# A decoder trunk: the second norm's steps directly behind the first's, one norm computed early, a normalization beside down products, and weights fetched by half units

## The chip, the cores and the metric

The kernel runs on one core of one Trainium2 chip. The metric is the time of one execution on the device in microseconds (us). TensorE (PE) multiplies matrices; VectorE (DVE), ScalarE (ACT) and GpSimd (POOL) work on elements; SyncE (SP) issues the DMAs. Each engine runs its own instructions in program order and waits where another engine's result is missing. Matrix products end up in PSUM, which has 8 banks here; everything else lies in SBUF. [...]

## The reference

One layer of a hybrid decoder, over 1072 positions (16 learned meta tokens, 1024 of the prompt, 32 of the samples), 1024 channels and a hidden width of 2816:

```python
def rmsnorm(x, g):
    y = xf * lax.rsqrt(jnp.mean(xf * xf, axis=-1, keepdims=True) + EPS)
    return (y * g.astype(jnp.float32)).astype(x.dtype)
...
def swiglu(x, wg, wu, wd):
    return (jax.nn.silu(x @ wg) * (x @ wu)) @ wd
...
    x = x + 0.5 * swiglu(rmsnorm(x, g1), w1g, w1u, w1d)
    h = rmsnorm(x, gm)
    z = h @ w_in + b_in
...
    x = x + jnp.concatenate([c, q], axis=-1) @ w_out + b_out
    x = x + 0.5 * swiglu(rmsnorm(x, g2), w2g, w2u, w2d)
```

Here c is a causal convolution over positions and q a pooling over several widths, both of z. A last norm follows.

## The kernel before

Channels lie on the partitions, positions along the rows. The positions are cut into three pieces of 358: X1, X2 and X3. Every value that is multiplied is split into a high part (a cast on ACT, `hi`) and the remainder (a subtraction, `lo`); a product is then three matmuls (high by high, low by high, high by low), which `mul` issues and `split` prepares. So every operand costs one ACT and one DVE (or POOL) instruction, and all weights go through ACT and POOL. In the rows, a name that ends in h or l is such a part (b11h, b11l).

TensorE's order is the order in which the program is written. `plan` is a list of steps: each takes its weights (`take`, `unit`) and issues products. Work of the other engines that doesn't belong to a step (norms, splits of operands, the mixing) is written as generators, which stand in a queue (`launch`); after each step some of their parts are issued, in order, and a part that ends in `yield LAG` lets that much of TensorE's time pass before the next. The order on DVE, ACT and POOL is then set by a scheduler, under the order of dependent work.

The stages:

1. Start (to about 80 us). The first two hidden tiles of FFN1 for X1 and X2 are computed before the norm is known: products run on x times the gain (`parts`, `product`), and the factor 1/rms is applied behind. Class `Start` writes this by hand. `rsqrt` is the norm: three column sums on TensorE (rows `ones,ns`), twelve tiny DVE instructions, a diagonal matrix `diag` on DVE, three matmuls with it that spread the factor over all partitions into a PSUM bank, and a copy `nr` of it. The products are named (0,0) to (0,3) for X1 and (1,0) to (1,3) for X2 (two of `g`, two of `u`). After them, `first_blocks`, `differences` and `last_blocks` make the seven operands b11 to b22 of the next stage.
2. FFN1 for X1 and X2 by "fast" blocks: seven products in place of eight, as in Strassen's scheme, on sums of weights (`block_steps`, tile `sx`) and sums of operands. Pairs of hidden tiles go through `fast_pass`; at pairs 1, 3, 5 and 7 groups of two pairs begin, whose down products (`fast_down`) are fast too, and whose ends load DVE heavily.
3. FFN1 for X3 (`plain_pass`, to about 850 us) and, with it, the first mixing. Its input is X3's norm (`rms`, 8 squares on ACT and 7 adds on DVE) and 8 scaled tiles in `normed` (tile `smt`).
4. FFN2 for X1's part (340 positions), with the second mixing between its steps, and from about 1260 us `fast_operands`: the norms of X2 and X3 and 60 DVE instructions that make the seven operands of
5. FFN2 for X2 and X3 by fast blocks, and the last norm.

Raw weights come by DMA in units of 512 KB (`raw_tile`, four buffers); `take` hands out a unit and keeps two more requested. A fast block uses two units: the first is split at once and kept; `sums` adds and subtracts the halves of both in four DVE instructions.

Of the kernel before, what the change touches and what calls it, by code (L numbers as in the profile page):

```python
# [13 lines left out]
P = 128  # L14
# [40 lines left out]
LAG4 = 7.0  # L55
POOL = {'b1': (1, 3), 't4': (0, 1, 2, 3), 't3': (0, 1, 2, 3), 't2': (1, 3), 'sq': ()}
W_BUFS = 6
T_BUFS = 6
R_BUFS = 4
# [22 lines left out]
def trunk(ctx: ExitStack, tc: tile.TileContext, xt, wf1, win, wout, wf2, wpool, vec, eye, sconv, spool,  # L82
# [64 lines left out]
    def raw_tile():  # L147
        return const.tile([P, KD, P], F32, name="wraw", tag="wraw", bufs=R_BUFS)

    def fetch(n):  # L150
        while len(fetched) < n and state["raw"] < len(raw_list):
            raw = raw_tile()
            for at, src in raw_list[state["raw"]]:
                to = at + src.shape[-1] // P
                nc.sync.dma_start(raw[:, at:to].rearrange("p k m -> p (k m)"), src)
# [15 lines left out]
    def unit(raw):  # L171
        return half_unit(raw[:, :KH]), half_unit(raw[:, KH:])
# [11 lines left out]
    def rsqrt(src, scale, add, out=None, copied=True):  # L184
# [22 lines left out]
        yield LAG2  # L207
# [63 lines left out]
    def fast_operands(pieces, gain, out):  # L271


        st = {}
# [7 lines left out]
        yield from rms(p0, st)  # L282
        yield from rms(p1, st)
        for k in range(KH):
            b11, b21, b12, b22, t3 = (temp()[:, :n] for _ in range(5))
            scaled(b11, p0, k, gain, st[p0])
            scaled(b21, p0, KH + k, gain, st[p0])
            yield
            put("b11", k, b11)
            put("b21", k, b21)  # L290
            yield
            scaled(b12, p1, k, gain, st[p1])
            scaled(b22, p1, KH + k, gain, st[p1])
            yield
            nc.vector.tensor_tensor(t3, b22, b12, ALU.subtract)
            nc.vector.tensor_tensor(b12, b12, b11, ALU.subtract)
            yield
            put("t1", k, b12)
            put("t3", k, t3)
            put("b22", k, b22)  # L300
            yield
            nc.vector.tensor_tensor(b22, b22, b12, ALU.subtract)
            put("t2", k, b22)
            yield
            nc.vector.tensor_tensor(b21, b21, b22, ALU.subtract)
            put("t4", k, b21)
            yield

    class Start:
# [4 lines left out]
        def __init__(self, pieces, gain, out, hid):  # L314
            self.pieces, self.gain, self.st = pieces, gain, {}
            self.n = pieces[0][1] - pieces[0][0]
            self.ops = out["ops"] = operand_tiles(self.n)
            self.accs, self.hid, self.sums, self.steps = {}, hid, {}, {}

# [25 lines left out]
        def norms(self, c):  # L345

            if c not in self.steps:
                self.steps[c] = rsqrt(self.sums[c], 1.0 / D, EPS)
                next(self.steps[c])
            else:  # L350
                self.st[c] = whole(self.steps[c])

        def after(self, c, j):

            if (c, j) == (0, 0):
                self.square_sums(0)
            elif (c, j) == (0, 1):
                self.norms(0)
                self.parts(1)
            elif (c, j) == (0, 2):  # L360
                self.square_sums(1)
            elif (c, j) == (0, 3):
                self.norms(0)
                self.outputs(0)
                self.first_blocks()
            elif (c, j) == (1, 0):
                self.norms(1)
            elif (c, j) == (1, 2):
                self.norms(1)
                self.differences()  # L370
            elif (c, j) == (1, 3):
                self.outputs(1)
                self.last_blocks()
                rest_of_start()

        def outputs(self, c):
            r = self.st[c]
            for i in range(2):
                t = pools["fast"].tile([P, self.n], F32, name="cc", tag="cc", bufs=4)
# [4 lines left out]
                if i not in self.hid:  # L384
                    fa1_places(0)
                split(self.hid[i][0][c], self.hid[i][1][c], t)
# [58 lines left out]
    def down_steps(wsrc, p, pieces, hid):  # L445
        out = []
        for j in range(2):
# [10 lines left out]
            out.append(("step", [source], lambda: unit(take()), use, False))  # L458
        return out

    def plain(src, use):
        return ("step", [[(0, src)]], lambda: unit(take()), use, False)
# [26 lines left out]
    def block_steps(src0, src1, product):  # L489
# [3 lines left out]
        def make0():  # L493
            st["r0"] = take()
            return unit(st["r0"])
# [5 lines left out]
        def sums():  # L501
            if "m5" not in st:
                r0, r1 = st["r0"], take()
                s1 = pools["fast"].tile([P, KH, P], F32, name="sx", tag="sx", bufs=2)
                nc.vector.tensor_tensor(s1, r1[:, :KH], r1[:, KH:], ALU.add)  # L505
                nc.vector.tensor_tensor(r1[:, :KH], r0[:, :KH], r1[:, :KH], ALU.subtract)  # L506
                nc.vector.tensor_tensor(r0[:, :KH], s1, r0[:, :KH], ALU.subtract)  # L507
                nc.vector.tensor_tensor(r0[:, KH:], r0[:, KH:], r0[:, :KH], ALU.subtract)
                st.update(m5=s1, m6=r0[:, :KH], m7=r1[:, :KH], m3=r0[:, KH:], m4=r1[:, KH:])
# [489 lines left out]
    r1b = {}  # L999
# [12 lines left out]
    def open_mix():  # L1012
# [10 lines left out]
        raw = raw_tile()[:, :C_TILES]  # L1023
# [36 lines left out]
    def fast_pass(pairs, downs, before, pieces, first):  # L1060
# [4 lines left out]
        for p, (g, u) in enumerate(pairs):  # L1065
# [24 lines left out]
            if p == 2:  # L1090
                do(launch, "twist", twist(pieces))
            elif p - 1 == last:
# [24 lines left out]
    def to_second_piece():  # L1117
# [3 lines left out]
        finish("h1b")  # L1121

    do(to_second_piece)
    put_down(fa1_d[PAIRS - 2])

# [6 lines left out]
    plain_pass(fb1, fb1_d, fa1_d[PAIRS - 1], {  # L1132
# [8 lines left out]
    def to_last():  # L1141
# [3 lines left out]
        launch("s2", fast_operands(FFN2_B, "g2", box["s2"]))  # L1145
# [5 lines left out]
            lambda: do(launch, "cb", mixer(MIX_B, lambda: both("small", n_b1, "sm"), box["cb"], lambda: cbs["b"]))],  # L1151
# [40 lines left out]
    def last_downs(c, j):  # L1192
# [19 lines left out]
        return ("step", raws, lambda: (unit(take()), unit(take())), use, False)  # L1212
# [17 lines left out]
    for p in steps:  # L1230
        raw_list.extend(p[1])
    raw_list[0] = [(at, raw_list[0][0][1][:, at * P : (at + KH) * P]) for at in (0, KH)]
# [4 lines left out]
    fetch(1)  # L1237
    for k in range(1, KD):
        start.load(0, k)
    fetch(2)  # L1240
    for k in range(KD):
        start.load(1, k)
        if k == 3:
            fetch(3)
# [111 lines left out]
```

## Time and profile before

| | |
|---|---|
| time, median of 3 runs | 1847.15 us (1845.55 to 1848.17) |
| the profiled execution | 1845.23 us, of which the span is 1843.5 us |
| busy: PE, DVE, ACT, POOL | 1747.4 us (95%), 1400.9 (76%), 761.2 (41%), 1154.1 (63%) |
| granted clock of TensorE, mean | 0.973 |

The span is the time from the first to the last recorded instruction. [...] A matmul of 358 columns is recorded with its whole passage (some 330 ns), while the next enters about 165 ns behind it.

### The profile page before, as it was taken

Reading aid. Unit: us, or ns where it says so; the run is one execution under the profiler, and the core shown is the slowest. Engines: PE = TensorE matmul, PEld = TensorE weight load, DVE = VectorE, ACT = ScalarE, POOL = GpSimd, SP = SyncE. Lnnn points to the kernel's source line nnn. Section 1 sums busy time; section 2 is a strip of 40 time slices with the busy share of each in tenths; the row PEclk is TensorE's granted clock in tenths of the full one; section 3 lists DMA queues with packets and bytes.
Section 4 is the critical chain, followed back from the end, with each engine's and each line's share of the span. In section 5 each row is a group of like instructions: output and inputs, shape, how many; then the busy total and the mean of one; then the engine's idle time right before and its main releaser. Section 6 shows DMA issues by size and latency. Waiting matters only on the chain.

```text
span 1843.5 us, 29182 instructions
## 1 busy us (share of the span) xinstructions
PE 1747.4 (95%) x10486; PEld 1726.9 (94%) x10486; DVE 1400.9 (76%) x2621; ACT 761.2 (41%) x1482; POOL 1154.1 (63%) x894
## 2 busy tenths in 40 slices
PE   8699999999899999999999999999799999999997
PEld 7699999999799999999999999999699899989997
DVE  8979797989746696898235888537878888797965
ACT  6434444444424324434235433535453434434344
POOL 6576766667635336667246658665577676766683
PEclk9799999999999999999999999999899999999998
DMA  6022222222243223343224493443233222222222
GB/s 204 24 74 78 78 69 69 79 73 95 97 91 119 76 70 101 129 135 118 69 93 136 120 139 127 137 137 120 87 92 94 74 70 69 82 77 72 69 92 87
DMA packets 74560, 176.17 MB, mean 96 GB/s; under 512 B 23728, under 2 KB 30128, under 8 KB 74416
## 3 DMA queue, kind: packets, MB, share of 16 engines
q1 hardware_dynamic: 74416, 174.31, 31.3%
q8 instruction: 83, 1.36, 0.3%
q14 instruction: 61, 0.50, 0.1%
HBM read 169.13 MB, written 5.15 MB: 95 GB/s over the span
## 4 chain that ended last, share of the span: by engine, by line
PE 72%; DVE 18%; issue 5%; DMA 3%; POOL 2%; ACT 1%; SPq 0%; DVEq 0%; POOLq 0%; ACTq 0%
PE acc L123 72%; DMA wraw<-in_wf 3%; POOL wl L141 2%; DVE acc L245 2%; DVE acc L535 1%; DVE wraw L506 1%; DVE tmp L535 1%; DVE acc L779 1%; DVE tmp L245 1%; DVE tmp L657 1%; DVE wraw L507 1%; DVE sx L505 0%; DVE x L456 0%; DVE dt4l L141 0%; DVE xk L245 0%
## 5 line engine op out<-in xcount | busy, mean ns | idle before, releaser
L141 POOL TENSOR_TENSOR wl<-wraw,wh 128x512 fp32r<-128x512 f32 x740 | 996.3, 1358 | 598.2 <-ACT wh L140 567.6
L140 ACT CAST wh<-wraw 128x512 fp32r<-128x512 f32 x740 | 453.9, 620 | 687.9 <-PE acc L123 465.6
L123 PE MATMUL acc<-smt,wh 128*128 128x358 f32 x1024 | 252.8, 328 | 4.5 <-DVE mixl L141 2.2
L123 PEld LDWEIGHTS acc<-smt,wh 128*128 128x128 f32 x1024 | 181.8, 190 | 5.8 <-DVE mixl L141 2.5
L779 DVE SCALAR_TENSOR_TENSOR acc<-ub,vecs,acc 128x340 f32<-128x340 f32 (+2 forms) x348 | 183.7, 573 | 2.7
L123 PE MATMUL acc<-mixlt,wh 128*128 128x340 f32 x704 | 167.0, 321 | 4.9 <-DVE smt L141 2.4
L123 PE MATMUL acc<-smt,wl 128*128 128x358 f32 x512 | 167.8, 328 | 0.0
L456 DVE SCALAR_TENSOR_TENSOR x<-acc,x 128x358 f32<-128x358 f32 (+1 forms) x240 | 119.5, 518 | 38.8 <-PE acc L123 38.1
L583 DVE SCALAR_TENSOR_TENSOR x<-acc,x 128x358 f32<-128x358 f32 x320 | 144.9, 518 | 0.2 <-PE acc L123 0.2
L123 PEld LDWEIGHTS acc<-mixlt,wh 128*128 128x128 f32 x704 | 121.9, 190 | 6.0 <-DVE smt L141 2.7
L535 DVE TENSOR_TENSOR acc<-tmp,acc 128x358 f32<-128x358 f32 x168 | 85.3, 527 | 51.3 <-PE acc L123 45.8
L141 POOL TENSOR_TENSOR wl<-sx,wh 128x512 fp32r<-128x512 f32 x58 | 86.0, 1484 | 49.1 <-ACT wh L140 46.8
L123 PE MATMUL acc<-mixlt,wl 128*128 128x340 f32 x352 | 112.8, 320 | 0.8 <-POOL wl L141 0.8
L123 PEld LDWEIGHTS acc<-smt,wl 128*128 128x128 f32 x512 | 96.9, 189 | 0.0
L505 DVE TENSOR_TENSOR sx<-wraw 128x512 f32<-128x512 f32 x58 | 62.4, 1076 | 38.5 <-DMA wraw<-in_wf 38.3
L507 DVE TENSOR_TENSOR wraw<-sx,wraw 128x512 f32<-128x512 f32 x58 | 78.7, 1357 | 9.8 <-POOL wl L141 9.7
L123 PE MATMUL acc<-mixh,wh 128*128 128x356 f32 (+1 forms) x320 | 79.9, 330 | 4.7 <-DVE mixl L141 2.7
L123 PE MATMUL acc<-mixl,wh 128*128 128x356 f32 (+1 forms) x320 | 79.1, 329 | 0.0
L123 PE MATMUL acc<-mixh,wl 128*128 128x356 f32 (+1 forms) x320 | 79.0, 329 | 0.0
L123 PE MATMUL acc<-xb,wh 128*128 128x358 f32 x256 | 65.9, 339 | 13.6 <-DVE tmp L535 9.6
L535 DVE TENSOR_TENSOR tmp<-tmp,acc 128x358 f32<-128x358 f32 x126 | 65.4, 519 | 13.2 <-PE acc L123 11.4
L482 DVE TENSOR_TENSOR acc<-acc,tmp 128x358 f32<-128x358 f32 (+1 forms) x44 | 23.2, 526 | 64.6 <-PE acc L123 51.2
(284 smaller groups left out, 4873.5 us busy)
## 6 DMA issues: line engine op xcount, KB each, us to landing
wraw<-in_wf SPq DMA_DIRECT2D x239, 512.0 KB, 3.3
wraw<-in_wf SPq DMA_DIRECT2D x66, 256.0 KB, 3.1
wraw<-in_win SPq DMA_DIRECT2D x24, 512.0 KB, 3.3
wraw<-in_wout SPq DMA_DIRECT2D x16, 512.0 KB, 3.3
x<-in_xt SPq DMA_DIRECT2D x8, 179.0 KB, 5.2
x<-in_xt SPq DMA_DIRECT2D x1, 1432.0 KB, 8.5
x<-in_xt SPq DMA_DIRECT2D x8, 178.0 KB, 4.6
out_yt<-tmp SPq DMA_DIRECT2D x8, 170.0 KB, 2.6
```

The costliest lines, as they stand in the source:

```text
L123: tc.keep_in_program_order(nc.tensor.matmul(acc, lhs, rhs, start=start, stop=stop))
L140: nc.scalar.copy(hi, src)
L141: (engine or nc.vector).tensor_tensor(lo, src, hi, ALU.subtract)
L245: nc.vector.scalar_tensor_tensor(t, X(k, piece), col(gain, k), r, ALU.mult, ALU.mult)
L456: nc.vector.scalar_tensor_tensor(X(m, piece), acc, 0.5, X(m, piece), ALU.mult, ALU.add)
L482: nc.vector.tensor_tensor(acc, acc, box["s"], ALU.mult)
L505: nc.vector.tensor_tensor(s1, r1[:, :KH], r1[:, KH:], ALU.add)
L506: nc.vector.tensor_tensor(r1[:, :KH], r0[:, :KH], r1[:, :KH], ALU.subtract)
L507: nc.vector.tensor_tensor(r0[:, :KH], s1, r0[:, :KH], ALU.subtract)
L535: nc.vector.tensor_tensor(t, s, acc, ALU.add)
L583: nc.vector.scalar_tensor_tensor(to, acc, 0.5 * sign, to, ALU.mult, ALU.add)
L779: nc.vector.scalar_tensor_tensor(to, src, w, part, ALU.mult, ALU.add)
```

## The change

Four things are changed. (A) In `Start`, the second norm's sums are issued directly behind the spread of the first, and its own spread two products earlier; the factor is read from the PSUM bank in which it was spread (`inbank`) where the other operand lies in SBUF; the gate of a product is finished in PSUM and the outputs are divided into smaller parts. (B) X3's norm is computed during FFN1's pair 4 from a second load of X3 through temporary tiles (`early_rms`); the normalization of X3 runs without `finish`, and the down products of the last two pairs both stand before the first plain step. (C) X2's norm for the last stage is launched before the end of the second mixing; `fast_operands` keeps one temporary in PSUM and pauses between its four rounds. (D) The raw weights come in units of 256 KB, eight buffers, up to five requested ahead; `sums` takes three such units.

```diff
-R_BUFS = 4
+R_BUFS = 8
+AHEAD = 5
...
-        return const.tile([P, KD, P], F32, name="wraw", tag="wraw", bufs=R_BUFS)
+        return const.tile([P, KH, P], F32, name="wraw", tag="wraw", bufs=R_BUFS)
...
         raw = fetched.popleft()
-        fetch(2)
+        fetch(AHEAD)
         return raw
...
+    def early_rms(piece, out):
+
+        a, b = piece
+        s = const.tile([P, N], F32, name="ns", tag="ns")[:, : b - a]
+        part = accum()[:, : b - a]
+        for k in range(KD):
+            t = temp()[:, : b - a]
+            nc.sync.dma_start(t, xt[:, k, a - PAD : b - PAD])
+            yield
+            if k == 0:
+                nc.scalar.activation(part, t, AF.Square)
+            else:
+                nc.scalar.activation(t, t, AF.Square)
+                nc.vector.tensor_tensor(s if k == KD - 1 else part, part, t, ALU.add)
+            yield
+        yield LAG5
+        out[piece] = yield from rsqrt(s, 1.0 / D, EPS, lag=LAG5)
...
         for k in range(KH):
-            b11, b21, b12, b22, t3 = (temp()[:, :n] for _ in range(5))
+            b11, b22, b21 = (temp()[:, :n] for _ in range(3))
+            t = accum()[:, :n]
             scaled(b11, p0, k, gain, st[p0])
+            scaled(b22, p1, KH + k, gain, st[p1])
+            yield
+            put("b11", k, b11)
+            put("b22", k, b22)
+            yield
+            scaled(t, p1, k, gain, st[p1])
+            t3 = temp()[:, :n]
+            sub(t3, b22, t, ALU.subtract)
+            sub(t, t, b11, ALU.subtract)
+            yield
+            put("t1", k, t)
+            put("t3", k, t3)
...
+            sub(t, b22, t, ALU.subtract)
+            put("t2", k, t)
+            put("b21", k, b21)
+            yield
...
+            sub(t, b21, t, ALU.subtract)
+            put("t4", k, t)
+            yield LAG6
...
             elif (c, j) == (0, 3):
                 self.norms(0)
-                self.outputs(0)
+                self.norms(1)
+                self.gate(0)
+                self.outputs(0, 0)
+                self.outputs(0, 1)
                 self.first_blocks()
             elif (c, j) == (1, 0):
                 self.norms(1)
-            elif (c, j) == (1, 2):
-                self.norms(1)
+            elif (c, j) == (1, 1):
+                self.gate(1)
                 self.differences()
...
-                nc.vector.tensor_tensor(t, t, r, ALU.mult)
-                nc.vector.tensor_tensor(t, self.accs[c, "u", i], t, ALU.mult)
...
+                nc.vector.tensor_tensor(t, t, self.inbank[c], ALU.mult)
...
-            scaled(t, self.pieces[c], k, self.gain, self.st[c])
+            scaled(t, self.pieces[c], k, self.gain, self.inbank[c])
...
+            (a11, a12), a21, a22 = st.pop("r0"), take(), take()
             s1 = pools["fast"].tile([P, KH, P], F32, name="sx", tag="sx", bufs=2)
-                nc.vector.tensor_tensor(s1, r1[:, :KH], r1[:, KH:], ALU.add)
+            nc.vector.tensor_tensor(s1, a21, a22, ALU.add)
...
+            elif p == 4 and first:
+                do(launch, "r1b", early_rms(FFN1_B, r1b))
...
-        launch("r1b", rms(FFN1_B, r1b))
...
-        finish("h1b")
 
     do(to_second_piece)
     put_down(fa1_d[PAIRS - 2])
+    put_down(fa1_d[PAIRS - 1])
...
+            lambda: do(launch, "r2", rms(FFN2_B[0], r2b))],
```

On TensorE, in the start, numbers behind a name tell buffers apart. Before, the sums of X2's norm (ns_323) and its spread (diag_487) stand apart: behind the first product of X2 (acc_445) come the sums and then the next product, and the spread stands behind the third.

```order
L123 MATMUL acc_382<-diag_268,ones_64 128x128 x3
L123 MATMUL acc_445<-t2h_88,wh_290 128x358
...
L123 MATMUL acc_445<-b22h_96,wl_295 128x358
L123 MATMUL acc_470<-ones_64,ns_323 128x1 x3
L123 MATMUL acc_501<-t2h_88,wh_349 128x358
...
L123 MATMUL acc_536<-b22h_96,wl_442 128x358
L123 MATMUL acc_561<-diag_487,ones_64 128x128 x3
L123 MATMUL acc_641<-t2h_88,wh_493 128x358
```

Now the sums (ns_338) follow the first spread (diag_281), and the second spread (diag_422) stands behind the first product of X2 (acc_485):

```order
L126 MATMUL acc_374<-b21h_86,wl_236 128x358
L126 MATMUL acc_399<-diag_281,ones_64 128x128 x3
L126 MATMUL acc_405<-ones_64,ns_338 128x1 x3
L126 MATMUL acc_485<-t2h_88,wh_303 128x358
...
L126 MATMUL acc_485<-b22h_96,wl_310 128x358
L126 MATMUL acc_510<-diag_422,ones_64 128x128 x3
L126 MATMUL acc_528<-t2h_88,wh_364 128x358
```

What moved: between the sums and the spread there were two products of 24 matmuls, and now there is one. The second bank, acc_510, is read by 14 instructions of DVE as the factor.

On VectorE, at the change of groups behind pair 4 (the one at 335 us of the profile), the order before is

```order
L508 TENSOR_TENSOR wraw<-wraw 128x512
L657 TENSOR_TENSOR tmp<-tmp,xb 128x358
L141 TENSOR_TENSOR dt4l_2406<-cc,dt4h_2404 128x358
L506 TENSOR_TENSOR wraw<-wraw 128x512
L535 TENSOR_TENSOR tmp<-tmp,acc 128x358
L141 TENSOR_TENSOR dt3l_1998<-tmp,hid2h 128x358
L535 TENSOR_TENSOR tmp<-tmp,acc 128x358 x2
L535 TENSOR_TENSOR acc<-tmp,acc 128x358 x3
```

and now, with the adds of the early norm (L259 in the new file, `acc<-acc,tmp`; L570, L541 and L543 there are L535, L508 and L506 here):

```order
L541 TENSOR_TENSOR wraw<-wraw 128x512
L692 TENSOR_TENSOR tmp<-tmp,xb 128x358
L259 TENSOR_TENSOR acc<-acc,tmp 128x358
L144 TENSOR_TENSOR dt4l_2473<-cc,dt4h_2471 128x358
L259 TENSOR_TENSOR acc<-acc,tmp 128x358
L144 TENSOR_TENSOR dt3l_2055<-tmp,hid2h 128x358
L570 TENSOR_TENSOR tmp<-tmp,acc 128x358
L259 TENSOR_TENSOR acc<-acc,tmp 128x358 x2
L543 TENSOR_TENSOR wraw<-wraw 128x512
L570 TENSOR_TENSOR tmp<-tmp,acc 128x358 x2
L570 TENSOR_TENSOR acc<-tmp,acc 128x358
L259 TENSOR_TENSOR acc<-acc,tmp 128x358 x2
```

What moved: the first `tmp<-tmp,acc` of the sums of products comes behind dt3l and two adds, and behind `wraw` no longer. At the other such places, which have no early norm, that row now stands one row earlier than before, ahead of dt4l, and `sx` three rows earlier.

On VectorE, at the end of `fast_operands`, the rows `acc<-acc,tmp` of 340 columns are the gate times up of a hidden tile, for whose split TensorE's next down products wait. Before:

```order
L482 TENSOR_TENSOR acc<-acc,tmp 128x340
L141 TENSOR_TENSOR t3l<-tmp,t3h 128x358
L302 TENSOR_TENSOR tmp<-tmp 128x358
L141 TENSOR_TENSOR t1l<-tmp,t1h 128x358
L305 TENSOR_TENSOR tmp<-tmp 128x358
L141 TENSOR_TENSOR hid2l<-acc,hid2h 128x340
L482 TENSOR_TENSOR acc<-acc,tmp 128x340
L141 TENSOR_TENSOR t2l<-tmp,t2h 128x358
L141 TENSOR_TENSOR t4l<-tmp,t4h 128x358
L456 SCALAR_TENSOR_TENSOR x_61<-acc,x_61 128x340
L141 TENSOR_TENSOR hid0l<-acc,hid0h 128x340
L456 SCALAR_TENSOR_TENSOR x_61<-acc,x_61 128x340 x7
```

Now (L515 is L482, L489 is L456):

```order
L144 TENSOR_TENSOR t4l<-acc,t4h 128x358
L515 TENSOR_TENSOR acc<-acc,tmp 128x340
L489 SCALAR_TENSOR_TENSOR x_61<-acc,x_61 128x340
L144 TENSOR_TENSOR t2l<-acc,t2h 128x358
L329 TENSOR_TENSOR acc<-tmp,acc 128x358
L489 SCALAR_TENSOR_TENSOR x_61<-acc,x_61 128x340
L144 TENSOR_TENSOR hid1l<-acc,hid1h 128x340
L489 SCALAR_TENSOR_TENSOR x_61<-acc,x_61 128x340 x3
L144 TENSOR_TENSOR t4l<-acc,t4h 128x358
L489 SCALAR_TENSOR_TENSOR x_61<-acc,x_61 128x340 x3
L515 TENSOR_TENSOR acc<-acc,tmp 128x340
L144 TENSOR_TENSOR hid2l<-acc,hid2h 128x340
```

What moved: before, the four remainders t3l, t1l, t2l and t4l of the fourth round stand behind the gate times up that is third from the end of this stage (the first row); now all of them stand ahead of it (it is the last row but one here), and t1, t2 and t4 are read from a PSUM bank `acc` in place of `tmp`.

## Rows read from the trace of the kernel before

**Rows 1.** The chain that ended last, 30 to 52 us (start us, us, what).
```profile
31.80 0.97 DVE cc L380 x2
...
34.95 5.57 DVE xk L245 x4
40.52 2.42 DVE cc L382 x2
```

**Rows 2.** TensorE's timeline, 40 to 90 us, with idle time before and its releaser.
```profile
51.55 1.65 PE L123 MATMUL acc<-diag,ones 128*128 128x128 f32 x6 [7.74 <-DVE diag L206]
53.75 0.67 PE L123 MATMUL acc<-t2h,wh 128*128 128x358 f32 x1 [0.55 <-ACT nr L215]
...
66.45 0.67 PE L123 MATMUL acc<-b11h,wh 128*128 128x358 f32 x1 [6.07 <-DVE cc L383]
...
78.36 0.44 PE L123 MATMUL acc<-dt1h,wh 128*128 128x358 f32 x1 [2.27 <-DVE tk L417]
```

**Rows 3.** Stretches of 20 us: start and end, busy us of each engine, PEclk, DMA.
```profile
40.00:60.00 20.00, 11.71 (x53) 11.12 (x52) 17.85 (x37) 5.75 (x12) 9.91 (x9) 0.74 0.07 25
80.00:100.00 20.00, 20.00 (x115) 20.00 (x114) 18.59 (x33) 6.90 (x13) 15.87 (x14) 0.92 0.01 3
460.00:480.00 20.00, 17.31 (x97) 16.75 (x97) 17.71 (x39) 8.03 (x16) 15.46 (x12) 0.91 0.32 102
500.00:520.00 20.00, 15.53 (x80) 15.38 (x81) 14.21 (x30) 6.64 (x15) 4.41 (x4) 0.83 0.17 54
1300.00:1320.00 20.00, 9.17 (x56) 8.53 (x54) 20.00 (x29) 9.68 (x21) 11.93 (x8) 0.80 0.31 105
1320.00:1340.00 20.00, 18.89 (x107) 18.90 (x108) 9.51 (x19) 5.25 (x11) 6.42 (x5) 0.86 0.15 53
```

**Rows 4.** What TensorE waited for in the whole run: us, times, longest.
```profile
PE acc L123 <- DVE tmp L535: 14.0, 15, 1.4
```

**Rows 5.** TensorE's timeline, 455 to 510 us.
```profile
470.65 0.83 PE L123 MATMUL acc<-ones,ns 128*128 128x1 f32 x6 [2.13 <-DVE ns L235]
```

**Rows 6.** TensorE's timeline, 500 to 506 us.
```profile
504.47 1.11 PE L123 MATMUL acc<-dt1h,wh 128*128 128x358 f32 x2 [6.19 <-DVE smt L141]
```

**Rows 7.** TensorE's timeline, 1286 to 1345 us.
```profile
1318.70 0.65 PE L123 MATMUL acc<-hid2h,wh 128*128 128x340 f32 x1 [10.18 <-ACT hid2h L140]
1321.11 0.65 PE L123 MATMUL acc<-hid2l,wh 128*128 128x340 f32 x1 [1.75 <-DVE hid2l L141]
```

**Rows 8.** VectorE by line and shape, 1265 to 1325 us (busy us, mean ns).
```profile
L245 DVE SCALAR_TENSOR_TENSOR tmp<-x,vecs,nr 128x358 f32<-128x358 f32 x16 | 13.5, 866 | 0.5 <-ACT nr L215 0.5
...
L141 DVE TENSOR_TENSOR t3l<-tmp,t3h 128x358 fp32r<-128x358 f32 x4 | 5.3, 1315 | 0.0
```

**Rows 9.** VectorE's timeline at one change of pair groups, 322 to 342 us.
```profile
335.37 0.52 DVE L141 TENSOR_TENSOR dt4l<-cc,dt4h 128x358 fp32r<-128x358 f32 x1
335.81 0.68 DVE L506 TENSOR_TENSOR wraw<-wraw 128x512 f32<-128x512 f32 x1
336.41 0.52 DVE L535 TENSOR_TENSOR tmp<-tmp,acc 128x358 f32<-128x358 f32 x1
336.85 1.41 DVE L141 TENSOR_TENSOR dt3l<-tmp,hid2h 128x358 fp32r<-128x358 f32 x1
```

**Rows 10.** TensorE's timeline at the same place, 333 to 345 us.
```profile
336.98 0.59 PE L123 MATMUL acc<-xb,wh 128*128 128x358 f32 x2 [1.41 <-DVE tmp L535]
```

**Rows 11.** The page: what the DMA engines moved, 40 slices of 46 us.
```profile
GB/s 204 24 74 78 78 69 69 79 73 95 97 91 119 76 70 101 129 135 118 69 93 136 120 139 127 137 137 120 87 92 94 74 70 69 82 77 72 69 92 87
```

**Rows 12.** The page: weight DMAs, KB each, us from issue to landing.
```profile
wraw<-in_wf SPq DMA_DIRECT2D x239, 512.0 KB, 3.3
wraw<-in_wf SPq DMA_DIRECT2D x66, 256.0 KB, 3.1
```

**Rows 13.** What VectorE waited for in the whole run.
```profile
DVE sx L505 <- DMA wraw<-in_wf: 38.3, 31, 6.7
```

More of the change, by code (lines that the diff above doesn't have):

```diff
@@ L182, in blocks, with rsqrt @@
         return [min(at, n - P) for at in range(0, n, P)]
-    def rsqrt(src, scale, add, out=None, copied=True):
+    def rsqrt(src, scale, add, out=None, copied=True, lag=LAG2):
         n = src.shape[-1]
@@ L269, in operand_tiles, with fast_operands @@
                 for name in OPERANDS}
-    def fast_operands(pieces, gain, out):
-        st = {}
+    def fast_operands(pieces, gain, out, stats):
+        st = stats
         p0, p1 = pieces
@@ L280, in put @@
             split(ops[name][0][:, k], ops[name][1][:, k], t)
-        yield from rms(p0, st)
-        yield from rms(p1, st)
+        for piece in pieces:
+            if piece not in st:
+                yield from rms(piece, st)
+        sub = nc.vector.tensor_tensor
         for k in range(KH):
-            b11, b21, b12, b22, t3 = (temp()[:, :n] for _ in range(5))
+            b11, b22, b21 = (temp()[:, :n] for _ in range(3))
+            t = accum()[:, :n]
             scaled(b11, p0, k, gain, st[p0])
+            scaled(b22, p1, KH + k, gain, st[p1])
[10 more added lines that the diff above has]
+            put("t3", k, t3)
             scaled(b21, p0, KH + k, gain, st[p0])
             yield
-            put("b11", k, b11)
+            sub(t, b22, t, ALU.subtract)
+            put("t2", k, t)
             put("b21", k, b21)
             yield
[L292 to L307, printed above, removed]
+            sub(t, b21, t, ALU.subtract)
+            put("t4", k, t)
+            yield LAG6
     class Start:
@@ L318, in __init__ @@
             self.accs, self.hid, self.sums, self.steps = {}, hid, {}, {}
+            self.out, self.inbank, self.gates = ({}, {}), {}, {}
         def place(self, c, k):
@@ L347, in norms @@
             if c not in self.steps:
-                self.steps[c] = rsqrt(self.sums[c], 1.0 / D, EPS)
+                self.steps[c] = rsqrt(self.sums[c], 1.0 / D, EPS, self.out[c])
                 next(self.steps[c])
@@ L351, in norms @@
                 self.st[c] = whole(self.steps[c])
+                self.inbank[c] = self.out[c]["psum"]
         def after(self, c, j):
@@ L493, in make0 @@
         def make0():
-            st["r0"] = take()
-            return unit(st["r0"])
+            st["r0"] = take(), take()
+            return tuple(half_unit(r) for r in st["r0"])
         def use0(w):
@@ L501, in sums @@
         def sums():
-            if "m5" not in st:
-                r0, r1 = st["r0"], take()
-                s1 = pools["fast"].tile([P, KH, P], F32, name="sx", tag="sx", bufs=2)
-                nc.vector.tensor_tensor(s1, r1[:, :KH], r1[:, KH:], ALU.add)
[L506 to L509, printed above, removed]
+            if "m4" in st:
+                return
+            (a11, a12), a21, a22 = st.pop("r0"), take(), take()
+            s1 = pools["fast"].tile([P, KH, P], F32, name="sx", tag="sx", bufs=2)
+            nc.vector.tensor_tensor(s1, a21, a22, ALU.add)
+            nc.vector.tensor_tensor(a21, a11, a21, ALU.subtract)
+            nc.vector.tensor_tensor(a11, s1, a11, ALU.subtract)
+            nc.vector.tensor_tensor(a12, a12, a11, ALU.subtract)
+            st.update(m5=s1, m6=a11, m7=a21, m3=a12, m4=a22)
         def made(name):
@@ L1210, in use @@
                     between(m)
[L1212 removed]
+        return ("step", raws, lambda: (unit(), unit()), use, False)
     def between(m):
@@ L1230, in trunk @@
     for p in steps:
-        raw_list.extend(p[1])
-    raw_list[0] = [(at, raw_list[0][0][1][:, at * P : (at + KH) * P]) for at in (0, KH)]
+        for _, src in sum(p[1], []):
+            raw_list.extend(src[:, at : at + KH * P] for at in range(0, src.shape[-1], KH * P))
     nc.sync.dma_start(vecs, vec)
     start.load(0, 0)
-    fetch(1)
+    fetch(2)
     for k in range(1, KD):
         start.load(0, k)
-    fetch(2)
+    fetch(4)
     for k in range(KD):
```

50 lines of the change are left out of this document (27 added, 23 removed).

## Prediction

> **What bounds the kernel now.** TensorE is busy 95% of the span, so only its idle stretches and the low clock behind them can be won. I went through its timeline for the gaps, asked of each what ended it, and then looked at what the releasing engine did in the meantime. Four places matter.
>
> The start: X1's factor reaches VectorE at 31.80, and from there it works without a pause through the eight xk tiles (four of them take 5.57 us) and two cc products (2.42) [rows 1]. X2's `diag`, the last piece of the second norm, stands behind all that, so TensorE waits 7.74 us for it, and later 6.07 us for a PSUM bank and 2.27 us for VectorE again [rows 2]. The granted clock is 0.74 between 40 and 60 us, and 0.92 between 80 and 100, where TensorE never idles [rows 3].
>
> The changes of pair groups: many small waits on the adds `tmp` of L535, 14.0 us in 15 waits, none over 1.4 [rows 4].
>
> Before FFN1 on X3: 2.13 us for X3's squares [rows 5], 6.19 us until its normalized tiles are split [rows 6], with clocks of 0.91 and 0.83 in the stretches around [rows 3].
>
> Before the last FFN: 10.18 and 1.75 us for a hidden tile's split [rows 7], while VectorE is busy 20.00 of 20 us with the seven operands [rows 3]. Its instructions on SBUF alone take long there: the `scaled` ones 866 ns, t3l 1315 ns in the mean [rows 8].
>
> **The change, part by part.** The sum is made against the profiled execution, 1845.2 us; the median is 1.9 us above it. Start-to-start times are read from VectorE's timeline: 0.44 us for a 358-column instruction, with or without a PSUM operand, but 1.33 us for dt3l, whose operands all lie in SBUF (recorded 1.41, less the 0.08 by which its neighbours' records overlap) [rows 9].
>
> *A, the start.* The instructions between X1's factor and X2's `diag` stay the same ones, 31.80 to 51.55 [rows 1, 2]. Cheaper are the xk and the cc that now read the factor from PSUM: four xk at 0.44 for 1.39 save 3.8, two cc at 0.44 for 1.21 save 1.5, the other four xk (34.95 less 32.77, 0.55 each) save 0.4. The cc now stand directly behind their Silu on ScalarE; I allow 1.0 for that wait. `diag` is ready at 46.9, 4.7 us earlier. But TensorE has two products less as cover. It went dry at 43.81 after three; a product of 24 matmuls runs 4.0 us, so now it does at 35.8, and waits 11.1 us in place of 7.74. The next product then runs at the low clock as X2's last one did (53.75 to 60.38, 6.6 us [rows 2]) and ends at about 54.3. VectorE's next gate waits for exactly that product, about 6 us, and in order with it everything behind. Then come the 33 instructions up to the last one that reads X2's factor from its bank: 33 × 0.44, and 2.0 for a few of the 1.33 us kind, make 16.5 us, to 70.8. The first product of the fast blocks takes this bank, and starts at 70.8 where it started at 66.45. Its 48 matmuls took 9.64 us (66.45 to 76.09), so the next begin at 80.4 and not at 78.36: 2.0 us lost. VectorE is further ahead by then, so the 2.27 us wait goes, and with it the 0.08 × 20 = 1.6 us of clock behind it [rows 3]. Net loss 0.4; because the longer idle stretches may also lower the clock longer, I take 1.5. Bounds: −2 (no wait for Silu, none of the 1.33 us kind) to +7 (six more of that kind, 0.89 each).
>
> *B, X3's norm early.* Removed: 2.13 and 6.19 of waiting, 0.09 × 20 = 1.8 us of clock, and of the 3.4 us in the second stretch the 2.6 that lie behind 504.47; together 12.7. The 8 scaled tiles and 8 splits, 16 × 0.44 = 7.0 us, now lie beside 192 down matmuls (31.7 us at 0.165), under which VectorE has 32 sums (14.1): hidden with 10 us to spare; without that cover they would cost the 7.0. Added: 8 DMAs, 8 squares on ScalarE (off the path), 7 adds on VectorE, which the scheduler put into the change of groups at 335 us, between results that TensorE waits for [rows 9, 10]. There VectorE has no slack, so 7 × 0.44 = 3.1 us is lost in full. The 13 small instructions of the norm lie beside the next down sums, free. Net −9.6; bounds −13 (adds hidden) to −6 (low clock added at 335 us).
>
> *C, the last FFN's operands.* The potential is 10.18 + 1.75, 0.14 × 20 = 2.8 us of clock and 0.6 before 1320 [rows 3, 7]: 15.3. To win it VectorE has to be about 12 us earlier. Of 60 instructions 28 now read PSUM; at 0.44 for a mean near 0.9 (between 866 ns [rows 8] and 0.44) they save about 13. X2's norm, launched in the mixing, takes at least 7 adds (3.1) from the stretch. So the late splits come early enough, and by the order the fourth round ends one hidden tile sooner. Between two gates without downs there stand 15 instructions still, 6.6 us at 0.44 or 10 with four of the 1.33 us kind, beside 48 matmuls (8 us): I leave 1.4 as a rest. Net −13.9; bounds −8 (rest of 7) to −15.3.
>
> [...]
>
> *D, half units.* At a change of groups TensorE waits for `tmp` of L535, 1.41 us at 336.98 [rows 10], behind dt4l and a `wraw` [rows 9]. In the new order this add stands one instruction, 0.44 us, earlier. Five such places without early squares: 2.2 us. VectorE's own wait for weights in `sums`, 38.3 us in 31 waits [rows 13], is mostly not under such a place, so I count no more. Bounds: 0, and −14.0 if all of L535's waits went. The DMAs themselves I count at nothing: the queue issues ahead.
>
> Sum: +1.5 − 9.6 − 13.9 − 2.2 = −24.2; 1845.2 − 24.2 + 1.9 = 1823 us.
>
> **The rivals.**
>
> *The start and the rest eat more (1834).* A at its bound of +7, C at −8: −12.8. For it: VectorE waits in order, and every long instruction counts. Against: each needs most of its instructions long.
>
> *Half units clear the group changes (1811).* D at −14. For it: a wait on a transfer at the head of a burst delays the whole burst. Against: the rows before the waits show work, not transfers [rows 9].
>
> *The early loads hold the weights (1847).* Their 8 DMAs go through six temporaries, in order with the weights on SyncE's queue; if VectorE's adds are late, so are weights. Eight landings at 3.1 us [rows 12], one behind another, are 25 us, less nothing that hides them: the gain is gone.
>
> *Half units hold TensorE back (slower).* A transfer of 256 KB takes 3.1 us where 512 KB takes 3.3 [rows 12]. Were halves carried out one behind another, they'd bring 256 KB / 3.1 us = 85 GB/s. The DMA engines carry up to 139 GB/s in slices of 46 us [rows 11]; beside the first, 21 slices lie above 85, and stretched to it they'd add about 300 us. It decides at about 125 GB/s, where seven slices above it (127 to 139) lengthen by 24 us together. Against: the 66 transfers of 256 KB there already come in pairs, and nothing stands still at them. [...]
>
> **How the numbers follow.** Chances: forecast 0.54, eaten 0.19, cleared 0.13, early loads 0.07, held back 0.07. The range leaves out the early loads, the held back and a little at the low end: 1808 to 1838. The likeliest case alone: 1814 to 1831. A difference of 0.2% (3.7 us) can be told from none here. Faster 0.87 (three cases and a little of the fourth), same 0.05, slower 0.08.
>
> **What would show it.** In the new profile: TensorE's wait for `diag` near 47 us of 10 to 13 us, then one of 6 to 8 us before the first b11h, and none before dt1h; no wait at X3's `ones,ns` and none before its first plain product; at 335 us waits about 3 us longer together; no 10 us wait before the last FFN, a clock of 1.00 there; the other group changes as they are, slightly shorter. It is wrong if `sums` wait longer for transfers (over 38 us), if SyncE's weights come late behind the early loads, or if the `scaled` instructions with a PSUM operand aren't near 0.44 us.

## The result and the profile after

The changed kernel takes 1805.15 us (median of 4 runs, 1803.07 to 1807.94), the kernel before, beside it, 1846.35 us: the ratio is 0.9779 with a 95% interval of 0.9761 to 0.9797. It is faster by 41 us, where 24 were forecast; 1805 lies under the range of 1808 to 1838.

The page of the changed kernel, its engines and what the DMA engines moved (slices of 45 us):

```profile
PE 1729.7 (96%) x10486; PEld 1712.5 (95%) x10486; DVE 1378.4 (77%) x2621; ACT 760.3 (42%) x1482; POOL 1146.0 (64%) x894
...
GB/s 209 35 83 71 71 103 82 72 77 98 103 118 119 65 67 115 124 135 111 66 106 129 126 135 133 126 134 123 111 105 91 71 83 71 82 71 72 70 100 83
...
wraw<-in_wf SPq DMA_DIRECT2D x544, 256.0 KB, 2.9
```

TensorE is busy 17.7 us less than before with the same number of matmuls; its mean granted clock, a share of the full one, rose from 0.973 to 0.986 (the records of both traces hold stretches of 1.00 and of 0.50, none between). The rest of the 42.2 us by which the span is shorter is idle time. Behind the first slice the DMA engines reach 135 GB/s (139 before [rows 11]), and a half unit lands in 2.9 us.

What TensorE waited for now:

```profile
PE acc L126 <- DVE diag L208: 11.1, 3, 7.5
PE acc L126 <- ACT wh L143: 11.0, 3, 9.3
...
PE acc L126 <- ACT cc L696: 5.8, 6, 1.2
...
PE acc L126 <- DVE smt L144: 2.9, 2, 2.4
...
PE acc L126 <- DVE tmp L570: 1.6, 2, 1.3
```

The two long waits on hidden tiles [rows 7] are not in the list; the wait for the adds `tmp` is 1.6 us in 2 for 14.0 in 15 [rows 4]; the longest on `smt` is 2.4 us for 6.19 [rows 6]. The 11.0 on `wh` is mostly one wait, in the start. There the timeline of TensorE reads:

```profile
45.38 1.65 PE L126 MATMUL acc<-diag,ones 128*128 128x128 f32 x6 [7.50 <-DVE diag L208]
...
69.54 0.64 PE L126 MATMUL acc<-b11h,wh 128*128 128x358 f32 x1 [9.26 <-ACT wh L143]
```

and stretches of 20 us (busy us of each engine, PEclk, DMA):

```profile
80.00:100.00 20.00, 20.00 (x124) 20.00 (x123) 13.07 (x24) 4.74 (x8) 15.09 (x14) 1.00 0.17 49
460.00:480.00 20.00, 20.00 (x123) 20.00 (x123) 12.10 (x23) 10.82 (x22) 17.31 (x13) 1.00 0.38 123
500.00:520.00 20.00, 20.00 (x124) 20.00 (x123) 10.13 (x22) 3.97 (x7) 7.20 (x7) 1.00 0.44 90
1240.00:1260.00 20.00, 17.33 (x102) 17.05 (x102) 20.00 (x42) 12.58 (x27) 12.26 (x10) 0.91 0.39 120
1300.00:1320.00 20.00, 18.99 (x118) 18.61 (x117) 9.30 (x16) 8.46 (x17) 13.05 (x10) 1.00 0.31 94
```

The clock is 1.00 in the stretches at 80, 460, 500 and 1300 us, where it was 0.92, 0.91, 0.83 and 0.80 [rows 3]. In the stretch at 1240 us it is 0.91 with VectorE busy throughout: a new wait.

Both programs have the same number of matmuls, so the traces can be laid beside each other by the n-th matmul, counted from 0. Start of the n-th in each trace (us); the last column is how much of the lead is won from line to line:

| n | place | before | after | lead | won |
|---|---|---|---|---|---|
| 400 | first fast pairs, start over | 99.56 | 99.12 | 0.4 | 0.4 |
| 800 | behind the first group of pairs | 172.18 | 165.71 | 6.5 | 6.0 |
| 2500 | behind the other groups of FFN1 | 462.44 | 452.44 | 10.0 | 3.5 |
| 2760 | first plain step on X3 | 518.16 | 496.30 | 21.9 | 11.9 |
| 7200 | before the last FFN's operands | 1259.16 | 1235.61 | 23.6 | 1.7 |
| 7600 | first products of the last FFN | 1338.51 | 1304.02 | 34.5 | 10.9 |
| 10485 | the last | 1834.81 | 1793.33 | 41.5 | 7.0 |

The span is 42.2 us shorter; the remaining 0.7 lies at the ends. Laid out by the same places, the forecast was −1.5, 0.4, −2.7 (0.4 less the 3.1 of the adds), 12.7, 0, 13.9 and 1.3. Two lines are short of the forecast, by 0.8 and 3.0 us. The surplus lies in the groups of the fast FFNs: 16.5 us won where the sum had a loss of 1. (The 1.7 us ahead of the last FFN differ from execution to execution: the repetition below loses 4.5 there.)

### The profile page after: what moved, and what is told of

Same layout as the page of the kernel before. It is cut to its first block, busy times and chain, and to the rows that moved or that the text cites. A ratio compares the mean times of both kernels' runs of the same rounds, so it can differ in the third digit from the quotient of the medians.

```text
span 1801.3 us, 29876 instructions
## 1 busy us (share of the span) xinstructions
PE 1729.7 (96%) x10486; PEld 1712.5 (95%) x10486; DVE 1378.4 (77%) x2621; ACT 760.3 (42%) x1482; POOL 1146.0 (64%) x894
## 4 chain that ended last, share of the span: by engine, by line
PE 75%; DVE 17%; issue 4%; DMA 2%; POOL 1%; ACT 1%; SPq 0%; DVEq 0%; POOLq 0%; ACTq 0%
PE acc L126 75%; DMA wraw<-in_wf 2%; DVE acc L265 2%; POOL wl L144 1%; DVE acc L814 1%; DVE wraw L542 1%; DVE acc L570 1%; DVE wraw L541 1%; DVE tmp L570 1%; DVE tmp L692 1%; DVE x L489 1%; DVE tmp L265 1%; DVE pr L832 1%; DVE wraw L543 0%; DVE xb L144 0%
## 5 line engine op out<-in xcount | busy, mean ns | idle before, releaser
L489 DVE SCALAR_TENSOR_TENSOR x<-acc,x 128x358 f32<-128x358 f32 (+1 forms) x240 | 119.4, 517 | 35.0 <-PE acc L126 34.2
L570 DVE TENSOR_TENSOR acc<-tmp,acc 128x358 f32<-128x358 f32 x168 | 85.7, 527 | 51.5 <-PE acc L126 48.2
L541 DVE TENSOR_TENSOR wraw<-wraw 128x512 f32<-128x512 f32 x58 | 77.0, 1327 | 0.4
L570 DVE TENSOR_TENSOR tmp<-tmp,acc 128x358 f32<-128x358 f32 x126 | 65.4, 519 | 14.3 <-PE acc L126 13.1
L126 PE MATMUL acc<-b11h,wh 128*128 128x358 f32 x184 | 61.7, 335 | 10.8 <-ACT wh L143 10.8
L543 DVE TENSOR_TENSOR wraw<-wraw 128x512 f32<-128x512 f32 x58 | 70.4, 1214 | 2.0 <-POOL wl L144 1.5
```

Source lines behind the costliest of these rows:

```text
L126: tc.keep_in_program_order(nc.tensor.matmul(acc, lhs, rhs, start=start, stop=stop))
L489: nc.vector.scalar_tensor_tensor(X(m, piece), acc, 0.5, X(m, piece), ALU.mult, ALU.add)
L541: nc.vector.tensor_tensor(a21, a11, a21, ALU.subtract)
L543: nc.vector.tensor_tensor(a12, a12, a11, ALU.subtract)
L570: nc.vector.tensor_tensor(t, s, acc, ALU.add)
```

## The experiments

The theory after the result: half units bring the weights for `sums` earlier (theory 1, the forecast's rival "half units clear the group changes"). Its rivals: the scheduler's new order alone (theory 2), and the greater depth of the requests (theory 3).

**Part D alone.** The kernel before with `raw_tile`, `take`, `unit`, `sums` and the fetches of the changed one.

```diff
-R_BUFS = 4
+R_BUFS = 8
+AHEAD = 5
...
-            st["r0"] = take()
-            return unit(st["r0"])
+            st["r0"] = take(), take()
+            return tuple(half_unit(r) for r in st["r0"])
```

> The kernel before with part D alone (256 KB units, eight buffers, up to five requested ahead). Theory 1, earlier arrival: half buffers come free sooner, so VectorE's sums of weights at the head of each burst no longer wait (38.3 us of waiting falls below 20) and every burst shifts with them: 1826 to 1833 us, most of TensorE's 14.0 us of waits on the adds tmp gone. Theory 2, order only: the scheduler merely puts the first add 0.44 us earlier at each of about six group changes: 1842 to 1845 us.

Measured: 1828.54 us, ratio 0.9901 (0.9884 to 0.9919). VectorE's waits for weights in the sums, and TensorE's for the adds:

```profile
DVE sx L507 <- DMA wraw<-in_wf: 12.4, 12, 5.9
```

```profile
PE acc L124 <- DVE tmp L537: 3.7, 2, 2.5
```

38.3 became 12.4 [rows 13], 14.0 became 3.7 [rows 4]. Theory 2 falls in the size given to it: D alone is worth 17 to 18 us, not 2 to 4. The new order is a part of D in every run, though, and wasn't tried by itself.

TensorE is busy 12.9 us less than before (1734.5 for 1747.4) and idle 4.9 us less: the greater part is the clock (0.982 in the mean for 0.973). The waits for the adds fell by 10.3 us, but others grew, those for the cast of `cc` from 4.3 to 7.4 us. In the changed kernel VectorE waits for weights about as little as with D alone:

```profile
DVE sx L540 <- DMA wraw<-in_wf: 14.1, 14, 4.9
```

**The changed kernel without D.** The same edit the other way.

> The changed kernel with part D undone (512 KB units, four buffers), A, B and C kept. Theory 1: 15 to 19 us slower than the changed kernel, 1820 to 1824 us, waits on weights in the sums back near 38 us. Theory 2: 2 to 4 us slower, 1807 to 1809 us. With theory 1 this is also where the forecast's sum without its term D should lie (1825).

Measured: 1820.51 us, ratio 0.9856 (0.9835 to 0.9877). The two views again:

```profile
DVE sx L538 <- DMA wraw<-in_wf: 43.5, 34, 5.8
```

```profile
PE acc L125 <- DVE tmp L568: 15.1, 16, 2.0
```

A, B and C together thus bring about 25.5 us by the medians, where their terms summed to 22.0. The greater part of the miss is D's.

**Depth or grain.** Four half units ahead in place of five in the changed kernel (`AHEAD = 4`); three full units ahead in place of two in the kernel before (`fetch(3)` in `take`).

> The changed kernel with four half units requested ahead in place of five, as many bytes as the two full units of the kernel before. If the finer grain of release and arrival gives the gain, nothing changes: 1803 to 1809 us. Theory 3, depth of the requests: a good part of the gain goes, 1815 us or more, and the sums wait for weights over 30 us.

> The kernel before with three full units requested ahead in place of two, in the same four buffers. Theory 3, depth: 1830 to 1838 us. Theory 1, grain: the buffers are what limits, not the number requested, 1844 to 1849 us.

Measured: 1803.59 us, ratio 0.9765 (0.9746 to 0.9784), and 1845.88 us, ratio 0.9998 (0.9979 to 1.0016). In the second, the sums wait as before:

```profile
DVE sx L505 <- DMA wraw<-in_wf: 38.2, 29, 6.6
```

```profile
PE acc L123 <- DVE tmp L535: 13.6, 15, 1.5
```

Theory 3 falls on both sides.

**Smaller transfers without smaller buffers.** The kernel before, each full unit by two DMAs.

```diff
-    raw_list[0] = [(at, raw_list[0][0][1][:, at * P : (at + KH) * P]) for at in (0, KH)]
+    raw_list[:] = [[(at + o, src[:, o * P : (o + KH) * P]) for at, src in e for o in range(0, src.shape[-1] // P, KH)]
+                   for e in raw_list]
```

> The kernel before with each full unit loaded by two DMAs of 256 KB into one buffer of 512 KB. It has part D's transfers without its release of half buffers. If the release is what brings the weights earlier, no change: 1843 to 1849 us and 35 to 40 us of waits in the sums. If smaller transfers alone do it, 1828 to 1835 us. If more transfers cost something, above 1850 us.

Measured: 1849.16 us, ratio 1.0000 (0.9987 to 1.0013).

```profile
DVE sx L505 <- DMA wraw<-in_wf: 42.5, 32, 6.6
```

```profile
PE acc L123 <- DVE tmp L535: 14.5, 17, 1.5
```

So it is not the size of the transfer (ratio 1.0000), nor how many are requested (0.9998). That the weights do come earlier with D can be counted from the loads that have landed when the n-th matmul starts. In the mean over n from 400 to 2500 these are 40.40 units of 512 KB in the kernel before, 40.41 with three units ahead and 40.42 with two loads per unit, but 40.97 with D alone and 40.84 in the changed kernel: half a unit more. What is left of part D, and what only it has, is that each half of a unit is a buffer of its own and comes free by itself, and the order of the instructions that follows from it. SyncE's queue shows what it waits for before it can issue a load, before and after:

```profile
SPq L155 <- POOL wl L141: 1583.7, 300, 23.1
```

```profile
SPq L156 <- POOL wl L144: 1057.2, 519, 29.8
SPq L156 <- DVE wraw L543: 378.5, 56, 13.1
```

In both it waits mostly for GpSimd's split of a raw weight, the last reader of a buffer: 5.3 us a wait with full units, 2.0 with half units, though there are more. With half units 56 waits of 6.8 us end with the last of VectorE's four sums (before, 3 waits of 16.9 us together ended with a sum): some halves now come free there. Both kinds together are 1436 us for 1601. A run in which the halves are buffers and are still released in pairs wasn't made, so the release is what remains, and isn't shown by itself.

**The other parts undone.** In the changed kernel, class `Start` of before; X3's norm and the order of before; `fast_operands` of before without the early norm of X2.

> The changed kernel with the start of before (part A undone). The forecast's term for A was a loss of 1.5 us: 1803 to 1804 us. By the shift between the two traces (0.4 us earlier at the 400th matmul) A is worth next to nothing: 1804 to 1807 us. If the start had helped the bursts behind it (VectorE further ahead), 1809 us or more.

> The changed kernel with part B undone (X3's norm at its old place, normalization ahead of the down products). The forecast's term: 9.6 us, so 1814 to 1816 us, of which 3.1 us were to be lost to the adds in the burst at 335 us. If these adds cost nothing now that the burst starts earlier, 12 to 13 us: 1817 to 1819 us.

> The changed kernel with part C undone. The forecast's term: 13.9 us, 1818 to 1820 us. By the shift between the traces (15.9 us won at the last FFN's start, some 5 us lost at a new wait about 60 us earlier): 10 to 12 us, 1815 to 1817 us.

Measured: 1813.13 us, ratio 0.9805 (0.9783 to 0.9828); 1819.75 us, 0.9841 (0.9820 to 0.9861); 1819.73 us, 0.9840 (0.9817 to 0.9863). Against the changed kernel's ratios (0.9779, and 0.9768 in a repetition below) A is worth about 5 to 7 us, B and C 11 to 13 each (each ratio's interval reaches some 4 us to either side). For A this is neither the forecast's loss nor the trace's nothing, but the third case of the expectation: the start helps what comes behind it. The place is the first group of pairs. The stretch from 100 to 120 us with the old start, with D alone, with A, B and C but not D, and in the changed kernel:

```profile
100.00:120.00 20.00, 17.03 (x90) 16.32 (x90) 12.27 (x16) 5.15 (x9) 15.57 (x13) 0.86 0.30 98
```

```profile
100.00:120.00 20.00, 16.33 (x99) 15.78 (x98) 11.73 (x16) 5.95 (x11) 16.00 (x14) 1.00 0.32 100
```

```profile
100.00:120.00 20.00, 18.28 (x111) 18.00 (x110) 12.79 (x21) 6.81 (x13) 14.87 (x12) 1.00 0.23 77
```

```profile
100.00:120.00 20.00, 20.00 (x123) 19.90 (x122) 16.97 (x25) 8.58 (x17) 15.30 (x12) 1.00 0.33 98
```

Here TensorE is busy throughout only with both, but one stretch says little: the repetition below has 18.7, near the 18.28 without D. The lead is steadier. From the 400th to the 800th matmul the lead on the kernel before grows by 1.4 us without D and by 1.0 with D alone, 0.9 is lost with the old start and all else changed, and in the eight traces that have both A and D it grows by 4.5 to 6.1. So some 2 to 5 us are in the price of A and in that of D, and the four prices add up to some 4 us more than the whole.

For B, the lead of the changed kernel on the one with the late norm is 0.0 us at the 1300th matmul (251.04 in both) and 0.3 at the 1820th (338.58 and 338.29), ahead of and behind the change of groups with the early norm: the seven adds cost nothing there.

**The changed kernel again, and three variants of it.** A pause of 10 between the rounds of the operands:

```diff
-LAG6 = 4.0
+LAG6 = 10.0
```

The last four scaled tiles of the start from the copy in SBUF:

```diff
-                self.put("b22", k, self.block(1, KH + k))
+                t = accum()[:, : self.n]
+                scaled(t, self.pieces[1], KH + k, self.gain, self.st[1])
+                self.put("b22", k, t)
```

and both with four half units ahead.

> The changed kernel once more, beside the next three on one chip: a ratio to the kernel before of 0.976 to 0.980. In its trace the wait on the cast of a weight near 1073 us is again under 1 us if the 3.6 to 4.1 us that three kernels with a part undone show there belong to their orders, and can be as long if it is chance of the execution.

> The changed kernel with a pause of 10 in place of 4 between the four rounds of the last FFN's operands (LAG6). If the waits at 1242 and 1265 us (2.67 and 1.31 us, with 1.7 us of low clock) come from rounds that follow each other too closely on VectorE, they go and nothing waits at the last FFN's start: 4 to 6 us faster than the changed kernel. If the operands then come too late, a wait appears at 1300 us, and it is no faster or slower.

> The changed kernel, in which the last four scaled tiles of the start (b22) read the factor from its copy in SBUF and not from the PSUM bank. The forecast had the first product of the fast blocks wait for the last reader of that bank. If so, it starts 3 to 5 us before 69.5 us and the kernel gains 2 to 4 us. If ScalarE's cast of its weights releases it, as the new profile has it, it starts at 68 to 70 us and nothing is gained.

> The changed kernel with the pause of 10, the earlier release of the bank and four half units ahead: the sum of what each brings, 1797 to 1802 us where the changed kernel has 1805; if the bank is not what is waited for, 1799 to 1802.

Measured: the changed kernel again 1806.43 us, ratio 0.9768 (0.9750 to 0.9787); the pause 1806.41, 0.9772 (0.9757 to 0.9788); the bank 1808.47, 0.9790 (0.9768 to 0.9812); all three 1805.88, 0.9770 (0.9753 to 0.9786). None beats the changed kernel.

The waits that the pause was to remove, in the changed kernel and with the pause:

```profile
1244.67 0.65 PE L126 MATMUL acc<-hid0h,wh 128*128 128x340 f32 x1 [2.67 <-DVE x L489]
...
1266.13 0.42 PE L126 MATMUL acc<-hid0l,wh 128*128 128x340 f32 x1 [1.31 <-DVE hid0l L144]
```

```profile
1250.96 0.42 PE L126 MATMUL acc<-hid0h,wh 128*128 128x340 f32 x1 [0.62 <-DVE x L489]
...
1275.57 0.42 PE L126 MATMUL acc<-hid2h,wh 128*128 128x340 f32 x1 [2.70 <-DVE x L489]
```

The first wait shrinks to 0.62, and a wait of 2.70 appears in the next group of down products, some 25 us later: the rounds now meet the down sums (L489) of that group, and the stall has moved. With the bank released earlier, TensorE's timeline in the start is

```profile
67.84 0.64 PE L126 MATMUL acc<-b11h,wh 128*128 128x358 f32 x1 [7.65 <-DVE tk L450]
...
73.11 0.67 PE L126 MATMUL acc<-b21h,wh 128*128 128x358 f32 x1 [1.35 <-DVE b22l L144]
```

The first product starts 1.7 us earlier, but the next then waits 1.35 for b22's split, which stands later on VectorE; the 280th matmul starts at 80.85 where it was 79.42. So the bank did hold the first product, by less than 2 us, and the next thing was right behind it.

The repetition shows a place that has nothing to do with the change. In the trace of the repetition and in that of the first run of the same kernel:

```profile
1076.96 0.94 PE L126 MATMUL acc<-mixlt,wh 128*128 128x340 f32 x2 [3.81 <-ACT wh L143]
```

```profile
1072.61 0.58 PE L126 MATMUL acc<-mixlt,wh 128*128 128x340 f32 x2 [0.20 <-ACT wh L143]
```

A weight's cast is late by 3.81 us in one execution and by 0.20 in the other. Waits of 3.3 to 5.6 us stand there in eight other traces too (3.6, 4.3 and 3.3 with the old start, the old norm and the old operands, 5.6 with two loads per unit), and of 1.5 in the kernel before. So they don't belong to these edits, and some 5 us of the lead at the 7600th matmul (34.5 in the first trace, 29.0 in the repetition) are a matter of the execution. What decides it stays open.

## Why the prediction was wrong

**The step that failed** is D: "VectorE's own wait for weights in `sums`, 38.3 us in 31 waits [rows 13], is mostly not under such a place, so I count no more." It was sized at 2.2 us and measures 17 to 18 alone, about 15 in the changed kernel (some 2 to 5 of them shared with A). The reasoning looked at the four instructions ahead of TensorE's wait [rows 9] and found work and no transfer. But VectorE is busy without a pause there; what makes it late lies ahead of these four, as far back as the head of the burst, more than 20 us earlier. In the kernel before, VectorE's timeline in the burst that ends at 165 us:

```profile
136.27 0.54 DVE L535 TENSOR_TENSOR acc<-tmp,acc 128x358 f32<-128x358 f32 x1 [2.77 <-PE acc L123]
...
142.05 1.50 DVE L505 TENSOR_TENSOR sx<-wraw 128x512 f32<-128x512 f32 x1 [1.12 <-DMA wraw<-in_wf]
143.47 0.52 DVE L535 TENSOR_TENSOR tmp<-tmp,acc 128x358 f32<-128x358 f32 x1
143.91 1.35 DVE L508 TENSOR_TENSOR wraw<-wraw 128x512 f32<-128x512 f32 x1
...
163.38 0.52 DVE L141 TENSOR_TENSOR dt4l<-cc,dt4h 128x358 fp32r<-128x358 f32 x1
...
164.42 0.52 DVE L535 TENSOR_TENSOR tmp<-tmp,acc 128x358 f32<-128x358 f32 x1
```

and the same instructions in the changed kernel, where dt4l stands behind the add:

```profile
133.00 0.54 DVE L570 TENSOR_TENSOR acc<-tmp,acc 128x358 f32<-128x358 f32 x1 [3.48 <-PE acc L126]
...
137.24 0.68 DVE L540 TENSOR_TENSOR sx<-wraw 128x512 f32<-128x512 f32 x1
137.84 0.52 DVE L570 TENSOR_TENSOR tmp<-tmp,acc 128x358 f32<-128x358 f32 x1
138.28 0.68 DVE L543 TENSOR_TENSOR wraw<-wraw 128x512 f32<-128x512 f32 x1
...
157.40 0.52 DVE L570 TENSOR_TENSOR tmp<-tmp,acc 128x358 f32<-128x358 f32 x1
157.83 1.20 DVE L144 TENSOR_TENSOR dt4l<-cc,dt4h 128x358 fp32r<-128x358 f32 x1
```

In both, the burst begins with a wait of VectorE for the same matmul, which comes 3.3 us earlier in the changed kernel (132.1 for 135.4, the 600th). Against that start, `sx` begins 1.5 us earlier (142.05 less 137.24, less 3.3), of which 1.12 is the wait for weights; it takes 0.68 us in place of 1.50; the `wraw` two rows on takes 0.68 in place of 1.35; and dt4l, 0.44 us, has moved behind the add, which is what the forecast counted for D. The add `tmp` for which TensorE waits, begun at 164.42 and 157.40, so comes 3.7 us earlier against that start. TensorE waited 1.40 us for it in the kernel before:

```profile
164.99 0.97 PE L123 MATMUL acc<-xb,wh 128*128 128x358 f32 x2 [1.40 <-DVE tmp L535]
```

The clock was 0.91 in the stretch from 160 to 180 us. Now TensorE doesn't wait for the add, and the clock is 1.00 there. Of the 3.7 us the wait for weights itself is less than a third. The two shorter sums bring 1.5 here, but nothing over the whole run, where the four sums take 274.8 us before and 274.0 with D alone. What D takes away over the run is the waiting, 38.3 to 12.4 us. The 3.3 us at the burst's head need A and D together: with D alone the 600th matmul comes 0.9 us later than before, without D 1.2 earlier. That a burst without slack passes its delay on to each wait behind it is argued from these rows; no run puts a wait of known length at the head of a burst. The rival "half units clear the group changes" said this ("a wait on a transfer at the head of a burst delays the whole burst"), and got 0.13; it should have been the forecast. Its price of 14.0 was too small as well: it counted the waits and not the low clock behind them. With D alone the time fell by 17 to 18 us, of which 12.9 are busy time of TensorE, while all of L535's waits were 14.0.

Its opposite, "half units hold TensorE back", falls with the same runs: with 544 transfers of 256 KB the slices behind the first reach 135 GB/s, and the ratio of the kernel that only splits the transfers is 1.0000. "The early loads hold the weights" falls too: with these loads in place the sums wait 14.1 us for weights, not over 38.

**A** went as worked out up to the end of the start, and was wrong in what it closed with. Three rows of VectorE there:

```profile
35.18 2.57 DVE L265 SCALAR_TENSOR_TENSOR xk<-x,vecs,acc 128x358 f32<-128x358 f32 x5
...
52.37 0.53 DVE L410 TENSOR_TENSOR cc<-acc,nr 128x358 f32<-128x358 f32 x1 [3.19 <-PE acc L126]
...
68.81 0.58 DVE L265 SCALAR_TENSOR_TENSOR acc<-x,vecs,acc 128x358 f32<-128x358 f32 x1
```

Five xk take 2.57 us, 0.51 each (0.44 forecast); `diag` releases TensorE at 45.38 (46.9), after 7.50 us and not 11.1 because TensorE's product had ended later than I placed it, at 37.9; the gate's product is waited for 3.19 us (6); the bank's last reader starts at 68.81 (70.4 by the forecast's count, 70.8 less 0.44), and b11h at 69.54 (70.8). The next matmuls come at 79.42 (80.4), without the old wait. Net 0.4 won; the worked value was a loss of 0.4, and 1.5 was taken. What the term left out is the lead of VectorE: "VectorE is further ahead by then" was used for one wait only. In the first group `sx` starts at 101.0 us in the changed kernel and at 104.0 with the old start, both behind a wait for weights (4.9 and 5.9 us), and between 100 and 120 us TensorE is busy 17.0 us with the old start, 20.0 and 18.7 in the two traces with the new one. That the lead passes through the weights, whose buffers come free earlier, is argued from these rows and not shown by a run of its own.

**B** was sized 12.7 gross and shows 11.9 in the trace; its 3.1 us for the adds at 335 us didn't come. Half units may have given VectorE slack at just that place, but this isn't shown: no run adds the squares alone, and the kernel that has them without half units passes from the 1300th to the 1820th matmul as fast as the kernel before (a lead of −1.1 us at the one, −1.0 at the other). **C** was sized 13.9 and shows 10.9: the 10.18 and 1.75 us waits are gone, as is the low clock, but 4.4 us of the potential stay unwon, not 1.4. They are a new wait of 2.67 for a down sum (L489) and one of 1.31 for a hidden tile's remainder, with the clock at 0.91, some 60 and 40 us ahead of the last FFN's first products; the forecast had a hidden tile between two rounds, the second kind alone. The saving by the PSUM operands was real but smaller than the sum had it. All four t4l in the stretch of the operands, before and now, and the four `scaled` instructions that only write to PSUM:

```profile
L141 DVE TENSOR_TENSOR t4l<-tmp,t4h 128x358 fp32r<-128x358 f32 x4 | 4.5, 1127 | 0.0
```

```profile
L144 DVE TENSOR_TENSOR t4l<-acc,t4h 128x358 fp32r<-128x358 f32 x4 | 2.1, 516 | 0.0
L265 DVE SCALAR_TENSOR_TENSOR acc<-x,vecs,nr 128x358 f32<-128x358 f32 x4 | 3.2, 846 | 0.0
```

The 28 instructions that now read PSUM took 23.5 us before and take 14.5, so 9.0 are saved where about 13 were counted. A `scaled` one gains nothing by writing to PSUM (846 ns, for 866 [rows 8]); in the start, where it reads the factor from PSUM, it takes 0.51 us. In the stretch of the operands an operand in PSUM made no instruction longer: the four t1l, with one, take 517 to 520 ns, and of the four b11l beside them, all in SBUF, three take 517 to 519 and one 987.

## What to carry to other kernels

Where an engine is saturated in a burst, price a wait at the head of the burst with all that stands behind it, not only with what stands next to the visible stall: the 38.3 us of waits for weights were counted at nothing, and with half units they fell to 12.4 and 17 to 18 us were won (that the delay is passed on is argued, not shown). A ring of buffers in smaller pieces was worth more here (ratio 0.9901) than more requests (0.9998) or smaller transfers (1.0000), though the release of the pieces wasn't tried by itself: ask what the queue waits for before it issues, and not how long a transfer takes. And parts that each remove one of two causes of the same stall have to be priced together: each alone brought about 1 us in the first group of pairs, both 4.5 to 6.

## What was not expected of the hardware

Splitting the transfers of 512 KB into two of 256 KB each (239 of them load `in_wf` [rows 12]) changed nothing that can be measured (ratio 1.0000, 0.9987 to 1.0013): the median from issue to landing is 3.1 us there, where it was 3.3 for a full one. And an all-SBUF addition of VectorE, `sx`, took 1.50 us before and 0.68 after at the same place in the program (what ran beside it wasn't varied). Over the run its mean fell from 1076 to 834 ns, while that of the `wraw` with two `wraw` operands on its next line (L506 before, L541 now) rose from 1158 to 1327.
